# Two-part float32r operands for the probabilities and values of a sparse attention branch

## The chip, the cores and the metric

The kernel runs on one core of one Trainium2 chip. The core has a matrix engine (PE; its weight loads are listed apart as PEld), a vector engine (DVE), a scalar engine (ACT), a general engine (POOL) and a sync engine (SP) that issues most DMA transfers. Each engine works through its own fixed list of instructions in order; between engines only semaphores order the work. The metric is the device time of one execution in microseconds (us); a profile of one further execution shows where the time goes.

## The reference

One decoder block over 512 tokens of width 1024: a modulated RMS norm, a wide input projection, two token mixers side by side (NSA, a sparse attention with three branches, and MLA, a latent attention), their gated merge, an output projection and a squared-ReLU MLP. The part that matters here is NSA: 8 heads in 2 groups of 4, head width 64, blocks of 128 queries, three softmax branches that each have their own keys and values, weighted by gates:

```
p_cmp = masked_softmax(s, dist_c >= 0)
o_cmp = jnp.einsum('bghqk,bgkd->bghqd', p_cmp.astype(vc.dtype), vc)
...
p = masked_softmax(s, smask[:, :, None])
o_sel = jnp.einsum('bghqk,bgqkd->bghqd', p.astype(vs.dtype), v_sel)
...
p = masked_softmax(s, wmask)
o_win = jnp.einsum('bghqk,bgkd->bghqd', p.astype(vw.dtype), v_win)
o = g[0] * o_cmp + g[1] * o_sel + g[2] * o_win
```

With 512 tokens the 8 selectable blocks of 64 keys are always all chosen and the window of 512 reaches back to the first token, so the second and third branch are both causal attention over all keys, with different keys and values. The compressed branch has 31 block keys and values, made by a small MLP (weights w_c1, w_c2) from the tokens.

## The kernel before, in words

Features lie on the partitions and tokens along the free axis. Every large product is written with operands split in two float32r parts (a rounded copy, made on ACT, and the remainder, made on DVE), as three matmuls of 512 columns: lines 197, 198 and 199 in `mm3`. A dense unit, `z_unit`, is 8 x 3 = 24 such matmuls into one of two PSUM banks `acc`.

The attention products do without this split for the probabilities. `nsa_scores(hl)` makes, for head `hl` of both groups, the scores of both causal branches (L543, L544, L550, L551), the softmax (DVE L344 adds the bias and takes the minimum, ACT L346 takes the exponential, `normalise` multiplies by the gated reciprocal: DVE L369, ACT L367). `nsa_values(hl, sc)` then, for each branch, transposes the probabilities of both groups on PE (L391, ten 128 x 128 transposes for one group and branch, into two PSUM banks `t`), copies them to SBUF on DVE (L379, tile `pT`, three buffers) and multiplies them with the values in plain float32 (L568). In a product the stationary operand is 64 columns wide; group 0 writes the upper 64 partitions of the single bank `o`, group 1 the lower 64. The trace has two records for one plain float32 matmul, and its names give 128*64 for one of these. The compressed branch has products of its own: `cmp_values` (L519, two matmuls of 512 columns in bank `m`, added to the head's output by DVE L521). The profile's L568 and L519 rows together are what I call the value products.

The program is written as a list of steps, `ORDER`; each letter is one function, a number its argument: `s1` is `nsa_scores(1)`, `v1` `nsa_values(1, ...)`, `w1` `cmp_values(1)`, `c` `cmp_softmax`, `h` `hidden` (the MLP of the compressed branch, L435), `g`, `q`, `k` dense units of gates and of MLA's latents, `p`, `a`, `b`, `m` the MLA steps. A scheduler then lays each engine's instructions out, earlier steps first, but lets later ones run ahead where buffers and inputs are there. Tiles of a pool with the same tag share a ring of buffers: `N` (20), `X` (8), `C` (3), `tmp` (5), `pT` (3), `p` (5, one per head, group and branch).

Of the kernel before, what the change touches and what calls it, by code (L numbers as in the profile page):

```python
# [10 lines left out]
F32R = mybir.dt.float32r  # L11
BF16 = mybir.dt.bfloat16
AF = mybir.ActivationFunctionType
ALU = mybir.AluOpType
PSUM = bass.MemoryType.PSUM

P = 128
S = 512
# [13 lines left out]
PB = dict(acc=2, s=2, t=2, o=1, m=1)  # L32
NB = dict(raw=4, hi=3, lo=3, p=5, pT=3, qst=2, tmp=5, N=20)
LJ = True
# [7 lines left out]
NA = ["1"]  # L42
ORDER = "f0 t0 s0 t1 f1 h v0 c s1 v1 s2 g1 v2 g1 q w0 s3 w2 v3 w1 k g1 p g1 g1 a1 w3 a0 b1 a2 e1 b0 a3 m1 b3 e1 m3 m0 g1 b2 m2"


@with_exitstack
def block_kernel(ctx: ExitStack, tc: tile.TileContext, d):
# [12 lines left out]

    big_a = slot("A", 16)    # modulated input, merged mixer output, modulated MLP input
    big_x = slot("X", 8)     # residual, attention outputs
    big_n = slot("N", NB["N"])    # attention operands, channel gates, MLP hidden
    small_c = slot("C", 3)
# [6 lines left out]

# [1 line left out]
    def wtile(shape=(P, 1024)):  # L73
# [38 lines left out]
    def scale_col(out, col, k, g):  # L112
        """(1 + scale) * gain, for a column of scales"""
        nc.vector.scalar_tensor_tensor(out[:, k:k + 1], mod[:, col:col + 1], badd[:, (k if g == C_GMIX else 8 + k):(k if g == C_GMIX else 8 + k) + 1],
                                       cols[:, g + k:g + k + 1], op0=ALU.add, op1=ALU.mult)
# [4 lines left out]

# [1 line left out]
    class Stats:  # L122
        """Sums of squares per token over feature tiles; the last tile goes straight to the tensor engine."""

# [23 lines left out]
        def rstd(self, tag="m", tag2="m", tok=ALL):  # L148
# [12 lines left out]
            nc.vector.reciprocal(r, s)  # L161
            # one Newton step for the square root: s <- s / 2 + (v / 2) / s
            nc.vector.tensor_tensor(v, v, r, op=ALU.mult)
# [6 lines left out]

# [1 line left out]
    def wsplit(src, shape, far=False):  # L172
# [33 lines left out]

# [1 line left out]
    for j, c0 in enumerate((0, 24)):  # L208
# [3 lines left out]
    st0 = Stats(KT)  # L212
    # the condition's row on all partitions
    pcs = [psum("t") for _ in range(2)]
# [3 lines left out]
    for k in range(KT):  # L218
        st0.add(xt[k], k == KT - 1)
        # keeps the tensor engine's clock up until the first projection  # L220
        if k in WARM:
            nc.tensor.matmul(warm, ones, xt[k], start=True, stop=True)
        if k in (CB0, CB0 + 1):
            j = k - CB0
            nc.scalar.activation(cb[:, j * S:(j + 1) * S], pcs[j], AF.Copy)
# [44 lines left out]

# [1 line left out]
    distm = big_n("distm")  # L272
# [5 lines left out]

    # keys: float32r parts of one group and both branches, each part on both halves of the partitions
    kh = [sb.tile([P, 2, S], F32R, name=f"kh{g}", tag="kk", bufs=4) for g in range(2)]  # L280
# [22 lines left out]

    # rope key, on all partitions: the sum of its two products
    rsel = sb.tile([64, P], F32, name="rsel", tag="rep", bufs=2)
# [5 lines left out]

    # gates, token-major: [tok, tile, 24]
    gates = sb.tile([P, NQ, 24], F32, name="gates")
# [12 lines left out]

    # values of the selected and window branches, token-major
    vt = {}

    def v_tiles(br):  # L330
        pz = z_unit(2 + br)
        zv = tmp("zv")
        nc.scalar.activation(zv, pz, AF.Copy)
        pt = psum("m")
        for kb in range(NQ):
            nc.tensor.transpose(pt[:, kb * P:(kb + 1) * P], zv[:, kb * P:(kb + 1) * P], ident)
        v = big_n(f"v{br}")
        nc.vector.tensor_copy(v, pt)
        vt[br] = v

# [1 line left out]
    def soft(pp, n, bias, scale, o, nm, sm):  # L342
        """exp of one row block: pp holds the negated scores"""
        nc.vector.tensor_tensor_reduce(out=o, in0=pp, in1=bias[:, S - n:S], scale=scale, scalar=3e38,  # L344
                                       op0=ALU.add, op1=ALU.min, accum_out=nm)
        nc.scalar.activation(o, o, AF.Exp, bias=nm, scale=-1.0, accum_out=sm)  # L346
# [34 lines left out]
    def p_transposed(aps):  # L381
        """P^T per key block: [keys, q from the block's first row on]"""
        out = [None] * NQ
# [14 lines left out]

# [1 line left out]
    def flat_tiles(b):  # L400
# [7 lines left out]
        for half in range(2):  # L408
            fl = big_n(f"flat{b}{half}").rearrange("p (m g b) -> p m g b", m=8, g=2)
            nc.gpsimd.memset(fl[:, :, :, 31:32], 0.0)  # L410
            for g in range(2):
                # token 16 b + 2 m for block b and pair m
                src = cz[g][:, 16 * half:16 * half + 496].rearrange("p (b m two) -> p m b two", b=31, two=2)
# [7 lines left out]
    kcp = sb.tile([P, 64], F32, name="kcp")  # L421
    vcp = big_n("vcp").rearrange("p (r c) -> p r c", r=4)
    hid = {}

    def hidden(fk, fv):
        """keys on the first 64 rows, values on the others: (kv, g, block) x 256"""
        nc.sync.dma_start(w2, d["w_c2"])
# [24 lines left out]
        for g in range(2):  # L452
            nc.scalar.activation(kcp[64 * g:64 * g + 64, 32 * g:32 * g + 32], pk[64 * g:64 * g + 64, 0:32],
                                 AF.Copy, scale=0.5)
        pv = psum("m")
        nc.gpsimd.memset(vcp, 0.0)
        for g in range(2):
# [6 lines left out]
        for r in range(4):  # L464
            nc.vector.tensor_scalar(vcp[32 * r:32 * r + 32, r], pv[32 * r:32 * r + 32, 0:P], 0.5, None,
                                    op0=ALU.mult)

    # compressed branch: softmax over the 31 blocks for all heads of a q tile
    pct = [None, None]

    def cmp_softmax():
        """all heads of two q tiles at a time; columns (q tile, hl, g, block)"""
        dc = [big_n(f"biasc{i}") for i in range(2)]
        for i in range(2):
            nc.sync.dma_start(dc[i], d["biasc"][i])
        for g in range(2):
            pct[g] = big_n(f"pct{g}")
        for ii in range(2):
            pp = psum("m")
            for i2 in range(2):  # L480
                i = 2 * ii + i2
                for hl in range(4):
# [18 lines left out]
                                    op=ALU.mult)  # L501
            # rows (g, hl, block) for the transposes
            pc = tmp("pc")
# [9 lines left out]
            for g in range(2):  # L513
                nc.vector.tensor_copy(pct[g][:, 256 * ii:256 * ii + 256], pt[:, 256 * g:256 * g + 256])

    def cmp_values(hl):
        po = psum("m")
        for g in range(2):
            nc.tensor.matmul(po[64 * g:64 * g + 64, :], vcp[:, hl, 64 * g:64 * g + 64], pct[g],  # L519
                             start=True, stop=True, skip_group_check=True)  # L520
        nc.vector.tensor_tensor(o_sp[hl], o_sp[hl], po, op=ALU.add)  # L521

# [1 line left out]
    o_sp = [None] * 8  # L524
# [37 lines left out]
    def nsa_values(hl, sc):  # L562
        po = psum("o")
        for br in range(2):
            tr = [p_transposed(sc[2 * g + br]) for g in range(2)]
            for kb in range(NQ):
                for g in range(2):
                    nc.tensor.matmul(po[64 * g:64 * g + 64, kb * P:],  # L568
                                     vt[br][:, kb * P + 64 * g:kb * P + 64 * g + 64], tr[g][kb],
                                     start=(br == 0 and kb == 0), stop=(br == 1 and kb == 3), skip_group_check=True)  # L570
        o_sp[hl] = big_x(f"o{hl}")
        evac(o_sp[hl], po)

# [1 line left out]
    zq, cq, ckv = [], [], []  # L575
# [81 lines left out]

# [1 line left out]
    tab = {}  # L659
# [13 lines left out]

    # columns of modb: (sc_a k, sh_a k) pairs, gt_a, (sc_m k, sh_m k) pairs, gt_m
    GTA, SCM, GTM = 16, 24, 40
# [12 lines left out]
    def ada_fill(end):  # L688
        """modulation columns up to pair end"""
        while ai[0] < min(end, 24):  # L690
            ada_late(ai[0])
            ai[0] += 1

    mqk, msc, lat = {}, {}, {}
    for step in ORDER.split():
# [15 lines left out]
        elif op == "c":  # L711
            cmp_softmax()
        elif op == "w":
            cmp_values(a)
        elif op == "p":
# [13 lines left out]

    # attention outputs in two parts, in the room of the keys and probabilities  # L730
    oh = []
# [12 lines left out]

# [1 line left out]
    nc.vector.tensor_scalar(modb[:, GTA:GTA + 8], modb[:, GTA:GTA + 8], 0.5, None, op0=ALU.mult)  # L746
# [21 lines left out]
    for n in range(KT - NH1):  # L768
# [3 lines left out]
        out_tile(n, pa, ALL)  # L772
    # the last tiles by halves of the tokens, so that the next norm of one runs beside the products of the other
    for k in range(KT):
# [18 lines left out]

# [1 line left out]
    st2 = Stats(KT, -1)  # L795
# [91 lines left out]
def _prep(inp):  # L887
# [4 lines left out]
    out["crow"] = asc(a["c"])  # L892
    # modulation columns: (sc_a, sh_a) by tile, gt_a, (sc_m, sh_m) by tile, gt_m
    order = []
# [70 lines left out]
```

## Time and profile before

| | |
|---|---|
| Median of 3 runs | 839.21 us (837.82 to 839.64) |
| Profiled execution, span from first to last instruction | 834.8 us |
| Median minus span | 4.4 us |
| PE busy in the span | 810.3 us (97%) |
| DVE busy | 494.0 us (59%) |
| ACT busy | 324.2 us (39%) |
| Granted PE clock | full in nearly every slice of the span |

The profile takes down one execution by itself, so the span is not the same thing as a run's time: 4.4 us lie around it. Busy PE time counts from a matmul's start to its modelled end, and matmuls overlap; how fast PE really goes is read from the distance of one start to the next. Times along the span are counted from its start.

### The profile page before, as it was taken

What the parts mean: (1) busy time and instruction counts of PE and PEld (TensorE: products, weight loads), DVE (VectorE), ACT (ScalarE), POOL (GpSimd) and SP (SyncE); (2) the same over time, 40 slices, a digit from 0 to 9 for tenths busy, and PEclk for the clock granted to TensorE, in tenths of its full rate; (3) what the DMA queues carried; (4) which work ended last, traced back from release to release, by engine and by line L of the source; (5) the groups of instructions that cost most, each with busy time, mean ns of one, the idle gap of its engine ahead of it and who ended that gap; (6) DMA issues with size and microseconds to landing.
All of it is one profiled execution on the core that took longest, in us unless ns stands there. A gap on an engine that the chain in (4) does not pass through costs nothing.

```text
span 834.8 us, 10364 instructions
## 1 busy us (share of the span) xinstructions
PE 810.3 (97%) x3916; PEld 631.5 (76%) x3916; DVE 494.0 (59%) x964; ACT 324.2 (39%) x572; POOL 88.2 (11%) x71
## 2 busy tenths in 40 slices
PE   6899999999999999999989999999999999999996
PEld 3687668665577656888769998888888888888885
DVE  6979668878658875468777745333333334333434
ACT  4458427465315543222333444224321342223431
POOL 2500000000000000003320013002200220012100
PEclk9999999999999999999999999999999999999998
DMA  9683251010041123487656203223333223333203
GB/s 348 237 278 114 95 184 51 26 51 26 26 149 54 51 78 119 158 285 239 207 177 226 102 26 121 87 97 102 101 101 97 87 94 101 102 101 100 78 1 101
DMA packets 30996, 99.66 MB, mean 119 GB/s; under 512 B 3521, under 2 KB 5761, under 8 KB 30946
## 3 DMA queue, kind: packets, MB, share of 16 engines
q1 hardware_dynamic: 30880, 98.89, 35.9%
q8 instruction: 31, 0.51, 0.2%
q14 instruction: 19, 0.16, 0.1%
q0 software_dynamic: 64, 0.11, 0.0%
q10 hardware_dynamic: 2, 0.00, 0.0%
HBM read 96.89 MB, written 2.10 MB: 119 GB/s over the span
## 4 chain that ended last, share of the span: by engine, by line
PE 83%; DVE 8%; DMA 4%; issue 2%; POOL 1%; ACT 1%; SPq 0%; DVEq 0%; POOLq 0%; ACTq 0%
PE ps_acc L197 14%; PE ps_acc L199 13%; PE ps_acc L198 13%; PE ps_s L197 8%; PE ps_s L198 7%; PE ps_s L199 7%; PE ps_t L391 4%; PE ps_o L568 3%; DVE junk L107 3%; DMA w_raw<-in_w_ada_dram 3%; PE ps_s L640 2%; PE ps_o L653 2%; POOL yb L758 1%; PE ps_acc L267 1%; PE ps_s L267 1%
## 5 line engine op out<-in xcount | busy, mean ns | idle before, releaser
L183 ACT ACTIVATE w_hi<-w_raw 128x1024 fp32r<-128x1024 f32 x105 | 111.0, 1059 | 293.1 <-PE ps_acc L198 158.3
L184 DVE TENSOR_TENSOR w_lo<-w_raw,w_hi 128x1024 fp32r<-128x1024 f32 x105 | 128.3, 1223 | 106.1 <-ACT w_hi L183 102.8
L198 PE MATMUL ps_s<-ul,w_hi 128*128 128x512 f32 (+1 forms) x264 | 99.4, 377 | 0.0
L197 PE MATMUL ps_s<-uh,w_hi 128*128 128x512 f32 (+1 forms) x264 | 99.4, 377 | 0.0
L199 PE MATMUL ps_s<-uh,w_lo 128*128 128x512 f32 (+1 forms) x264 | 99.3, 376 | 0.0
L197 PE MATMUL ps_acc<-h2h,w_hi 128*128 128x512 f32 x224 | 87.1, 389 | 0.0
L198 PE MATMUL ps_acc<-h2l,w_hi 128*128 128x512 f32 x224 | 87.1, 389 | 0.0
L199 PE MATMUL ps_acc<-h2h,w_lo 128*128 128x512 f32 x224 | 87.1, 389 | 0.0
L828 POOL TENSOR_TENSOR relu<-relu 128x512 f32<-128x512 f32 x32 | 48.4, 1515 | 308.6 <-ACT relu L823 296.8
L798 DVE SCALAR_TENSOR_TENSOR xr<-ps_s,modb,xr 128x512 f32<-128x512 f32 (+1 forms) x35 | 24.7, 705 | 95.0 <-PE ps_s L199 94.9
L198 PE MATMUL ps_acc<-hl,w_hi 128*128 128x512 f32 x200 | 80.1, 401 | 0.0
L199 PE MATMUL ps_acc<-hh,w_lo 128*128 128x512 f32 x200 | 80.0, 400 | 0.0
L197 PE MATMUL ps_acc<-hh,w_hi 128*128 128x512 f32 x200 | 79.4, 397 | 0.0
L346 ACT ACTIVATE p<-p,nm 128x128 f32<-128x128 f32 (+3 forms) x96 | 53.3, 556 | 58.1 <-DVE nm L344 56.9
L379 DVE COPY pT<-ps_t 128x512 f32<-128x512 f32 (+1 forms) x72 | 42.4, 598 | 30.6 <-PE ps_o L568 16.1
L198 PEld LDWEIGHTS ps_s<-ul,w_hi 128*128 128x128 f32 x264 | 49.7, 188 | 9.5 <-DVE ul L829 0.4
L197 PEld LDWEIGHTS ps_s<-uh,w_hi 128*128 128x128 f32 x264 | 49.7, 188 | 9.2 <-DVE xr L798 0.2
L199 PEld LDWEIGHTS ps_s<-uh,w_lo 128*128 128x128 f32 x264 | 49.7, 188 | 9.0
L107 DVE SCALAR_TENSOR_TENSOR junk<-w_raw,cb 128x1024 bf16<-128x1024 f32 x32 | 40.1, 1254 | 14.7 <-DMA w_raw<-in_w_ada_dram 14.6
L198 PEld LDWEIGHTS ps_acc<-h2l,w_hi 128*128 128x128 f32 x224 | 42.0, 188 | 8.8
L197 PEld LDWEIGHTS ps_acc<-h2h,w_hi 128*128 128x128 f32 x224 | 42.0, 188 | 8.7
L199 PEld LDWEIGHTS ps_acc<-h2h,w_lo 128*128 128x128 f32 x224 | 42.0, 188 | 8.7
(387 smaller groups left out, 1458.1 us busy)
## 6 DMA issues: line engine op xcount, KB each, us to landing
w_raw<-in_w_fc_dram SPq DMA_DIRECT2D x64, 512.0 KB, 3.4
w_raw<-in_w_ada_dram SPq DMA_DIRECT2D x32, 512.0 KB, 4.2
w_raw<-in_w_z_dram SPq DMA_DIRECT2D x25, 512.0 KB, 3.7
w_ada<-in_w_ada_dram SPq DMA_DIRECT2D x16, 512.0 KB, 5.7
w_raw<-in_w_c_dram SPq DMA_DIRECT2D x8, 512.0 KB, 3.9
w_raw<-in_w_o_dram SPq DMA_DIRECT2D x8, 512.0 KB, 4.2
w_raw<-in_w_out_dram SPq DMA_DIRECT2D x8, 512.0 KB, 3.5
w_raw<-in_w_g_dram SPq DMA_DIRECT2D x8, 448.0 KB, 6.5
```

The source lines that it names most:

```text
L107: nc.vector.scalar_tensor_tensor(junk, w, 1.0, cb, op0=ALU.mult, op1=ALU.mult, accum_out=mod[:, col:col + 1])
L183: nc.scalar.activation(hi[:, :n], raw[:, :n], AF.Copy)
L184: nc.vector.tensor_tensor(lo[:, :n], raw[:, :n], f(hi[:, :n]), op=ALU.subtract)
L197: nc.tensor.matmul(out, w[0], x[0], start=first, stop=False)
L198: nc.tensor.matmul(out, w[0], x[1], start=False, stop=False)
L199: nc.tensor.matmul(out, w[1], x[0], start=False, stop=last)
L346: nc.scalar.activation(o, o, AF.Exp, bias=nm, scale=-1.0, accum_out=sm)
L379: nc.vector.tensor_copy(dst, src)
L391: nc.tensor.transpose(pp[:, off:off + P], aps[i][:, kb * P:(kb + 1) * P], ident)
L568: nc.tensor.matmul(po[64 * g:64 * g + 64, kb * P:], vt[br][:, kb * P + 64 * g:kb * P + 64 * g + 64], tr[g][kb], start=(br == 0 and kb == 0 ...
L798: nc.vector.scalar_tensor_tensor(xt[n][:, tok], pa[:, tok], modb[:, GTM + n:GTM + n + 1], xt[n][:, tok], op0=ALU.mult, op1=ALU.add)
L828: nc.gpsimd.tensor_tensor(r2, r, r, op=ALU.mult)
```

## The change

The probabilities and the values of the NSA branches now go through float32r as well. Each transposed probability tile is split in two parts, `pTh` by ACT and `pTl` by DVE (L423 and L424 of the new file), the values of each branch and group are kept as one tile in which the two parts of V lie side by side (64 + 64 columns per key block), and a product is two float32r matmuls with a stationary operand of 128 columns: one for `pTh`, one for `pTl` (L602). The upper half of the output bank holds the sums with V's first part, the lower half those with its second. The compressed branch's probabilities are split the same way and are added in the same accumulation (L606), so that `cmp_values` and the `w` steps are gone. At the end ACT copies the lower half out and DVE adds the upper (L610, L611). A group has a whole bank to itself now, so the single bank `o` is used once for each head and group (eight times) instead of once for each head pair. `c` moves ahead of `v0`. `pT` gets four buffers, and a split tile takes two of them; `N` gets 19. Comments are taken out as well.

```diff
-NB = dict(raw=4, hi=3, lo=3, p=5, pT=3, qst=2, tmp=5, N=20)
+NB = dict(raw=4, hi=3, lo=3, p=5, pT=4, qst=2, tmp=5, N=19)
-ORDER = "f0 t0 s0 t1 f1 h v0 c s1 v1 s2 g1 v2 g1 q w0 s3 w2 v3 w1 k g1 p g1 g1 a1 w3 a0 b1 a2 e1 b0 a3 m1 b3 e1 m3 m0 g1 b2 m2"
+ORDER = "f0 t0 s0 t1 f1 h c v0 s1 v1 s2 g1 v2 g1 q s3 v3 k g1 p g1 g1 a1 a0 b1 a2 e1 b0 a3 m1 b3 e1 m3 m0 g1 b2 m2"
+    def value_parts(name, src, get):
+        v = get(name, F32R)
+        v4 = v.rearrange("p (kb part c) -> p kb part c", part=2, c=64)
+        nc.scalar.activation(v4[:, :, 0], src, AF.Copy)
+        nc.vector.tensor_tensor(v4[:, :, 1], src, f(v4[:, :, 0]), op=ALU.subtract)
+        return v
...
-        v = big_n(f"v{br}")
-        nc.vector.tensor_copy(v, pt)
-        vt[br] = v
+        src = pt.rearrange("p (kb g c) -> p kb g c", kb=NQ, g=2)
+        vt[br] = []
+        for g in range(2):
+            vt[br].append(value_parts(f"v{br}{g}", src[:, :, g], big_n))
...
+    def p_parts(aps):
+        out = [None] * NQ
+        for grp in ((0,), (1, 3), (2,)):
+            pp = psum("t")
...
+            th = sb.tile([P, S], F32R, name="pTh", tag="pT", bufs=NB["pT"])
+            tl = sb.tile([P, S], F32R, name="pTl", tag="pT", bufs=NB["pT"])
+            nc.scalar.activation(th[:, :off], pp[:, :off], AF.Copy)
+            nc.vector.tensor_tensor(tl[:, :off], pp[:, :off], f(th[:, :off]), op=ALU.subtract)
...
-    vcp = big_n("vcp").rearrange("p (r c) -> p r c", r=4)
+    vc = [small_c(f"vc{g}", F32R) for g in range(2)]
...
+        for g in range(2):
+            v4 = vc[g].rearrange("p (r part c) -> p r part c", r=4, part=2)
+            src = vcp[:, :, 64 * g:64 * g + 64]
+            nc.scalar.activation(v4[:, :, 0], src, AF.Copy)
+            nc.vector.tensor_tensor(v4[:, :, 1], src, f(v4[:, :, 0]), op=ALU.subtract)
...
-                nc.vector.tensor_copy(pct[g][:, 256 * ii:256 * ii + 256], pt[:, 256 * g:256 * g + 256])
+                to, of = slice(256 * ii, 256 * ii + 256), pt[:, 256 * g:256 * g + 256]
+                nc.scalar.activation(pct[g][0][:, to], of, AF.Copy)
+                nc.vector.tensor_tensor(pct[g][1][:, to], of, f(pct[g][0][:, to]), op=ALU.subtract)
...
     def nsa_values(hl, sc):
-        po = psum("o")
-        for br in range(2):
-            tr = [p_transposed(sc[2 * g + br]) for g in range(2)]
-            for kb in range(NQ):
-                for g in range(2):
-                    nc.tensor.matmul(po[64 * g:64 * g + 64, kb * P:],
-                                     vt[br][:, kb * P + 64 * g:kb * P + 64 * g + 64], tr[g][kb],
-                                     start=(br == 0 and kb == 0), stop=(br == 1 and kb == 3), skip_group_check=True)
         o_sp[hl] = big_x(f"o{hl}")
-        evac(o_sp[hl], po)
+        for g in range(2):
+            po = psum("o")
+            for br in range(2):
+                tr = p_parts(sc[2 * g + br])
+                for kb in range(NQ):
+                    for t in tr[kb]:
+                        nc.tensor.matmul(po[:, kb * P:], vt[br][g][:, kb * P:(kb + 1) * P], t,
+                                         start=(br == 0 and kb == 0 and t is tr[0][0]), stop=False,
+                                         skip_group_check=True)
+            for t in pct[g]:
+                nc.tensor.matmul(po, vc[g][:, hl * P:(hl + 1) * P], t, start=False, stop=(t is pct[g][1]),
+                                 skip_group_check=True)
+            r = slice(64 * g, 64 * g + 64)
+            u = tmp("osum")
+            nc.scalar.activation(u[r], po[64:P], AF.Copy)
+            nc.vector.tensor_tensor(o_sp[hl][r], po[0:64], u[r], op=ALU.add)
```

The scheduler lays the engines' lists out anew. On PE, in the values of the second head pair (`v1`), the list before had this (`v_794` is the second branch's values, `kh` and `kl` keys, `ident` the identity of a transpose; the scores are the third pair's):

```order
L391 MATMUL ps_t<-ident,p 128x128 x2
L568 MATMUL ps_o<-pT,v_794 64x512
L391 MATMUL ps_t<-ident,p 128x128 x8
L550 MATMUL ps_s<-kh_509,qst 128x512
L551 MATMUL ps_s<-kl_511,qst 128x512
L543 MATMUL ps_s<-kh_510,qst 128x256
L544 MATMUL ps_s<-kl_512,qst 128x256
L391 MATMUL ps_t<-ident,p 128x128 x2
L568 MATMUL ps_o<-pT,v_794 64x512
L568 MATMUL ps_o<-pT,v_794 64x384
```

In the same place of the new list stand these (`v_641` is the first branch's values of group 0):

```order
L419 MATMUL ps_t<-ident,p 128x128 x7
L602 MATMUL ps_o<-pTh,v_641 128x512
L419 MATMUL ps_t<-ident,p 128x128 x2
L602 MATMUL ps_o<-pTl,v_641 128x512
L602 MATMUL ps_o<-pTh,v_641 128x384
L602 MATMUL ps_o<-pTl,v_641 128x384
L602 MATMUL ps_o<-pTh,v_641 128x256
L419 MATMUL ps_t<-ident,p 128x128 x4
L602 MATMUL ps_o<-pTl,v_641 128x256
L602 MATMUL ps_o<-pTh,v_641 128x128
L602 MATMUL ps_o<-pTl,v_641 128x128
```

A product for `pTh` follows ACT's copy, the next for `pTl` follows DVE's remainder, and only transposes stand between them. From the last product of the first head's group 0 to the last of the third head pair the new list holds five dense matmuls, all at the start; the list before has 63 dense matmuls from the first product of `v1` to the last of `v2`.

ACT takes the results of dense units out of the two `acc` banks. In the list before, the first latent unit `cqz` leaves its bank (L583, and L130 for its squares) ahead of the softmax of the fourth head pair (`qn_535`):

```order
L367 ACTIVATE p<-p,rc 128x256 x2
L183 ACTIVATE w_hi<-w_raw 128x1024
L583 ACTIVATE cqz_1601<-ps_acc 128x512
L130 ACTIVATE sq<-ps_acc 128x512
L346 ACTIVATE p,sm<-p,nm 128x128 x2
L346 ACTIVATE p,sm<-p,nm 128x256 x2
L346 ACTIVATE p,sm<-p,nm 128x384 x2
L346 ACTIVATE p,sm<-p,nm 128x512
L534 ACTIVATE qst<-qn_535 64x512
```

In the new list it leaves after the last `osum` of the third head pair:

```order
L423 ACTIVATE pTh<-ps_t 128x512
L356 ACTIVATE p,sm<-p,nm 128x384
L423 ACTIVATE pTh<-ps_t 128x512
L423 ACTIVATE pTh<-ps_t 128x256
L356 ACTIVATE p,sm<-p,nm 128x512 x2
L610 ACTIVATE osum<-ps_o 64x512
L622 ACTIVATE cqz_1771<-ps_acc 128x512
L130 ACTIVATE sq<-ps_acc 128x512
L622 ACTIVATE cqz_1806<-ps_acc 128x512
L130 ACTIVATE sq<-ps_acc 128x512
```

Both banks `acc` hold latent units until then.

## Rows read from the trace of the kernel before

**Rows 1.** The page's head: span, then busy time, share, instructions per engine.
```profile
span 834.8 us, 10364 instructions
...
PE 810.3 (97%) x3916; PEld 631.5 (76%) x3916; DVE 494.0 (59%) x964; ACT 324.2 (39%) x572; POOL 88.2 (11%) x71
...
PEclk9999999999999999999999999999999999999998
```
**Rows 2.** The page's chain that ended last, share by engine.
```profile
PE 83%; DVE 8%; DMA 4%; issue 2%; POOL 1%; ACT 1%; SPq 0%; DVEq 0%; POOLq 0%; ACTq 0%
```
**Rows 3.** Stretches: length, busy us per engine, granted clock, DMA share, GB/s.
```profile
92.30:226.85 134.55, 133.57 (x711) 86.44 (x711) 100.47 (x282) 65.47 (x154) 4.43 (x8) 1.00 0.21 71
147.70:163.70 16.00, 15.87 (x90) 9.23 (x89) 12.47 (x40) 6.72 (x22) 0.00 (x0) 1.00 0.09 30
```
**Rows 4.** PE in order of time: start, length, record; the value products.
```profile
149.62 1.07 PE L568 MATMUL ps_o<-pT,v 128*64 128x512 f32 x4
150.62 0.44 PE L550 MATMUL ps_s<-kh,qst 128*128 128x384 f32 x1
...
151.48 0.86 PE L568 MATMUL ps_o<-pT,v 128*64 128x384 f32 x4
152.27 0.66 PE L391 MATMUL ps_t<-ident,p 128*128 128x128 f32 x4
...
162.12 0.86 PE L568 MATMUL ps_o<-pT,v 128*64 128x256 f32 x6
162.91 1.09 PE L391 MATMUL ps_t<-ident,p 128*128 128x128 f32 x8
```
**Rows 5.** The same view: float32r matmuls of 512, 384 and 256 columns.
```profile
157.91 0.28 PE L543 MATMUL ps_s<-kh,qst 128*128 128x256 f32 x1
158.03 0.28 PE L544 MATMUL ps_s<-kl,qst 128*128 128x256 f32 x1
...
161.44 0.34 PE L550 MATMUL ps_s<-kh,qst 128*128 128x384 f32 x1
161.62 0.34 PE L551 MATMUL ps_s<-kl,qst 128*128 128x384 f32 x1
161.79 0.40 PE L198 MATMUL ps_acc<-hl,w_hi 128*128 128x512 f32 x1
...
164.31 0.39 PE L198 MATMUL ps_acc<-hl,w_hi 128*128 128x512 f32 x1
164.54 0.39 PE L199 MATMUL ps_acc<-hh,w_lo 128*128 128x512 f32 x1
```
**Rows 6.** Groups by line and shape: count, busy us, mean ns, idle before.
```profile
L379 DVE COPY pT<-ps_t 128x512 f32<-128x512 f32 x48 | 32.8, 687 | 25.0 <-PE ps_o L568 12.5 <-PE ps_t L391 7.2 <-PE ps_o L653 4.7
...
L346 ACT ACTIVATE p<-p,nm 128x512 f32<-128x512 f32 x24 | 17.2, 718 | 8.4 <-DVE nm L344 8.1
...
L344 DVE CUSTOM_DVE_ANT_0 p<-ps_s,distm 128x512 f32<-128x512 f32 x16 | 10.8, 686 | 1.7 <-PE ps_s L551 1.7
...
L289 DVE TENSOR_TENSOR kl<-ps_t,kh 64x512 fp32r<-64x512 f32 x8 | 5.5, 686 | 0.1
...
L287 ACT ACTIVATE kh<-ps_t 64x512 fp32r<-64x512 f32 x8 | 4.7, 590 | 0.1
```
**Rows 7.** DVE in order of time: a copy of 256 columns and what follows.
```profile
161.23 0.42 DVE L379 COPY pT<-ps_t 128x256 f32<-128x256 f32 x1 [0.35 <-PE ps_o L568]
161.57 1.00 DVE L369 TENSOR_SCALAR p<-p,rc 128x128 f32<-128x128 f32 x3
```
**Rows 8.** Waits from 92.3 to 226.85: us in total, times, longest.
```profile
PEld ps_o L568 <- DVE pT L379: 3.2, 8, 0.6
...
PEld ps_t L391 <- DVE pT L379: 1.5, 4, 0.8
```
**Rows 9.** The w_c1 products' matmuls, shortest, median, longest ns, first and last start.
```profile
L435 PE MATMUL ps_m<-w_raw,flat x64: 379/379/431, 92.3 to 107.7; 128*64 128x256 f32 x64
```
**Rows 10.** The chain from 92 to 109 us: start, length, what.
```profile
96.96 3.95 DMA w_raw<-in_w_c_dram
```

More of the change, by code (lines that the diff above doesn't have):

```diff
@@ L397, in p_transposed @@
         return out
+    def p_parts(aps):
+        out = [None] * NQ
+        for grp in ((0,), (1, 3), (2,)):
+            pp = psum("t")
+            off = 0
+            pos = []
+            for kb in grp:
+                pos.append(off)
+                for i in range(kb, NQ):
+                    nc.tensor.transpose(pp[:, off:off + P], aps[i][:, kb * P:(kb + 1) * P], ident)
+                    off += P
+            th = sb.tile([P, S], F32R, name="pTh", tag="pT", bufs=NB["pT"])
+            tl = sb.tile([P, S], F32R, name="pTl", tag="pT", bufs=NB["pT"])
+            nc.scalar.activation(th[:, :off], pp[:, :off], AF.Copy)
+            nc.vector.tensor_tensor(tl[:, :off], pp[:, :off], f(th[:, :off]), op=ALU.subtract)
+            for kb, o in zip(grp, pos):
+                out[kb] = [t[:, o:o + (NQ - kb) * P] for t in (th, tl)]
+        return out
     def flat_tiles(b):
@@ L455, in hidden @@
         pv = psum("m")
+        vcp = tmp("vcp").rearrange("p (r c) -> p r c", r=4)
         nc.gpsimd.memset(vcp, 0.0)
@@ L476, in cmp_softmax @@
         for g in range(2):
-            pct[g] = big_n(f"pct{g}")
+            pct[g] = [big_x(f"pct{part}{g}", F32R) for part in "hl"]
         for ii in range(2):
@@ L513, in cmp_softmax @@
             for g in range(2):
-                nc.vector.tensor_copy(pct[g][:, 256 * ii:256 * ii + 256], pt[:, 256 * g:256 * g + 256])
-    def cmp_values(hl):
-        po = psum("m")
-        for g in range(2):
-            nc.tensor.matmul(po[64 * g:64 * g + 64, :], vcp[:, hl, 64 * g:64 * g + 64], pct[g],
-                             start=True, stop=True, skip_group_check=True)
-        nc.vector.tensor_tensor(o_sp[hl], o_sp[hl], po, op=ALU.add)
+                to, of = slice(256 * ii, 256 * ii + 256), pt[:, 256 * g:256 * g + 256]
+                nc.scalar.activation(pct[g][0][:, to], of, AF.Copy)
+                nc.vector.tensor_tensor(pct[g][1][:, to], of, f(pct[g][0][:, to]), op=ALU.subtract)
     o_sp = [None] * 8
@@ L562, in nsa_values @@
     def nsa_values(hl, sc):
-        po = psum("o")
-        for br in range(2):
-            tr = [p_transposed(sc[2 * g + br]) for g in range(2)]
-            for kb in range(NQ):
-                for g in range(2):
-                    nc.tensor.matmul(po[64 * g:64 * g + 64, kb * P:],
-                                     vt[br][:, kb * P + 64 * g:kb * P + 64 * g + 64], tr[g][kb],
-                                     start=(br == 0 and kb == 0), stop=(br == 1 and kb == 3), skip_group_check=True)
-        o_sp[hl] = big_x(f"o{hl}")
-        evac(o_sp[hl], po)
+        o_sp[hl] = big_x(f"o{hl}")
+        for g in range(2):
[14 more added lines that the diff above has]
+            nc.vector.tensor_tensor(o_sp[hl][r], po[0:64], u[r], op=ALU.add)
     zq, cq, ckv = [], [], []
@@ L712, in block_kernel @@
             cmp_softmax()
-        elif op == "w":
-            cmp_values(a)
         elif op == "p":
```

## The prediction

> **What bounds the kernel now.** I read the page's head first: PE is busy 97% of the span at full granted clock, DVE 59%, ACT 39% [rows 1]. The chain that ended last runs over PE for 83% of its length [rows 2]. Then the stretches. The value products of NSA lie between the first w_c1 product (L435, 92.30) and the first product of MLA's w_uv (226.85), 134.55 us in which PE is busy 133.57, DVE 100.47 and ACT 65.47 [rows 3]. Inside `v1` it is the same: PE 15.87 of 16.00, DVE 12.47, ACT 6.72 [rows 3].
>
> A busy PE may still be slack, so I priced its instructions from one start to the next in the time-ordered view of `v1`. A float32r matmul takes 0.23 at 512 columns (164.31 to 164.54), 0.18 at 384 (161.44 to 161.62), 0.12 at 256 (157.91 to 158.03) [rows 5]; a transpose 0.11, from (1.09 - 0.66) / 4 [rows 4]. A plain float32 product of 512 columns takes 1.00 (149.62 to 150.62), a pair that starts with 384 columns 0.79, one that starts with 256 columns 0.79 [rows 4]. Going into and out of such a block costs besides: the matmul that follows it has a record of 0.44 where one of its shape has 0.34 [rows 4, 5], and the block at 162.12 starts 0.33 after a 512-column matmul that should take 0.23 [rows 4, 5]. So 0.19 a block for both. At these prices all work of the stretch comes to 128.7 of its 134.55 us, and 5.8 are stalls: PE does bound it.
>
> The Trainium skill (Perfetto Trace Analysis, section Identifying the Most-Contended Engine) would have me judge PE by its busy weight loads, not by matmuls. They are 86.44 of 134.55, 64% [rows 3], below DVE's 75%; by that DVE is the bound and the change, which leaves DVE's work as it is, gives nothing: 839. The pitches speak against it. It is part of rival B.
>
> **The change part by part.** *Removed on PE.* For one head pair and branch the products take 1.00 + 1.00 + 0.79 + 0.80 = 3.59; eight of these are 28.7. L519 gives five blocks of 1.00 in the stretch, 5.0. The list has 36 blocks, x 0.19 = 6.9. Sum 40.6; two more L519 blocks stand behind the stretch, 2 x 1.19 = 2.4. Removed: 43.0.
>
> *Added on PE.* For one head, group and branch: two parts of four matmuls, 2 x (0.228 + 0.175 + 0.121 + 0.11) = 1.27; sixteen make 20.3. The compressed branch adds 16 x 0.228 = 3.6. Sum 23.9. No row shows float32r at 128 columns: a quarter of 0.23 is 0.06, and the 256-column price 0.12 is the other bound. I take the transpose's 0.11; the 32 matmuls move the sum by -1.7 to +0.3. PE's net: 43.0 - 23.9 = 19.1 us less.
>
> *DVE.* Where it copied `pT` (687 ns for 512 columns) it now subtracts, and a subtraction from PSUM of that size takes 686 [rows 6]: nothing. Eight `osum` additions (0.69) take the place of four copies of `o` and four additions of L521: nothing.
>
> *ACT.* New are 32 copies of 512 columns at 0.59 (L287 [rows 6]), 16 of 256 at about 0.34 (a little over half), 8 `osum` at 0.59 and some 3 us for V and the compressed probabilities: 18.9 + 5.4 + 4.7 + 3 = 32 us. ACT goes from 65 to 97 in the stretch, below PE. No cost by itself, as long as the queues don't cross.
>
> *Where they do cross.* I cut the new PE list at the same marks into five pieces and priced each.
> - A, the w_c1 products with group 0 of `v0`: PE 12.9. But the weights set this piece: a transfer of 3.95 us stands on the chain at 96.96 [rows 10], and the products run from 92.3 to 107.7 [rows 9]. 15.7 as before.
> - B, `c`, scores and 91 dense matmuls: PE 29.9, DVE 28, ACT 21. With about half the old stalls 33.
> - C, the rest of `v0` with all of `v1` and `v2`: 86 transposes, 92 value products, 34 scores and five dense matmuls, PE 32.4. DVE: 28 remainders and 6 additions, 18 x 0.69 + 10 x 0.42 + 6 x 0.69 = 20.8 [rows 6, 7]; 26 masks, 0.69 at 512 columns and in proportion below, 12; 15 multiplications at about 0.4, 6; small ones 6. The records add up to 45, but neighbours overlap: a copy of 0.42 starts at 161.23 and the next instruction at 161.57, 0.08 before its end [rows 7]. Some 90 such places take off 7: DVE 38. ACT 33.5. So C is no longer PE's: DVE decides. No dense work covers it, since both `acc` banks hold latent units until ACT reaches L622. At each of six head ends PE stops, ACT takes 0.59 for `osum`, and DVE waits for that: 6 x 0.6 = 3.6. C is 42.
> - D, 72 dense matmuls with `v3`: PE 30.1, DVE 23, ACT 23; with the other half of the stalls 32.
> - E, the way to w_uv: PE 6.8, taken as 7.3.
>
> Sum 130.0. The same work took 134.55 + 2.4 = 136.9. So -6.9: PE's 19.1 lose 12 to the places where DVE, ACT or a transfer is late next.
>
> *Edits at nothing.* `N` 19: the MLP behind needs fewer. `pT` 4: the MLA steps share it and had three. The C ring: `vc0` and `vc1` hold two of its three buffers until `v3` is done, so SP's qt_rope transfers wait, and behind them the later weights; the uqk loads stand ahead in SP's queue and some 25 us of dense work cover them. Without that cover it costs a transfer, 4 us [rows 10]; I keep that for the upper end. The single bank `o`, used eight times in place of four: the bank is free after ACT 0.59 + DVE 0.69, with 0.8 us of transposes between; in C that is within DVE's time.
>
> The profiled execution is 834.8, the median 4.4 above it. 834.8 - 6.9 + 4.4 = 832.3 us.
>
> **Rivals.**
> *A: all of PE's saving arrives.* For it: DVE has 34 us of room in the stretch and the softmax of the next pair can run ahead of the values. Against: in C only five dense matmuls stand, and DVE's 38 alone are over PE's 32.4. With C at 36 and B, D without stalls the sum is 15.7 + 30 + 36 + 30.1 + 7 = 118.8, -18.1: 821.1.
>
> *B: nothing changes.* For it: if DVE and ACT, not PE, set the pace in C (at 48 to 49), the piece eats the saving: 88.0 + 48.9 = 136.9. Also if the changed products cost more than by the pitches. Against: before, DVE was the one that waited, its 512-column copies 12.5 us for L568 and 7.2 for transposes [rows 6]. 839.
>
> *C: slower, by the hand-over in piece C.* Each split group is a chain: four transposes (0.44), ACT's `pTh` (0.59), DVE's `pTl` (0.69), and only then the last product and a free buffer. Before, one copy stood there (0.69), and PE had dense matmuls to run meanwhile. If nothing overlaps, 18 groups of 512 columns take 1.72 and 10 of 256 take 0.22 + 0.34 + 0.42 = 0.98: 40.8. On each of the two engines stand softmax instructions ahead (0.72 and 0.69 at 512 columns [rows 6], some 0.45 over all widths); half of one on each adds 0.45 per group, 12.6. C is 53.4, the sum 141.4, +4.5: 843.7. It decides from 48.9, that is from (48.9 - 40.8) / 28 = 0.29 us of queueing per group without any overlap. For it: ACT waited 8.1 for DVE's `nm` and DVE 1.7 for scores [rows 6], so these queues already cross. Against: there are two banks `t`, so that one group's transposes run beside another's copies, and before PE waited for `pT` only 3.2 us in 8 places at the products and 1.5 in 4 at the transposes [rows 8].
>
> The Trainium skill (Perfetto Trace Analysis, section Optimization Strategy) says that a gap which repeats on the engine that should be full can mean too few buffers. The trace of before shows it only in those 4.7 us; after, a split group holds two of four `pT`, so the rule would back this rival.
>
> **How the numbers follow.** About 0.2% (1.7 us) is what a measurement of this kernel can tell from no change: 837.5 to 840.9. The forecast, with C from 37 to 47, has 0.55 and its own range 824 to 837.5; A 0.13; B 0.13; C 0.19, spread from 841 upward. Faster: 0.55 + 0.13 = 0.68; same 0.13; slower 0.19. A's lower half and C's upper half are left out: the range is 820 to 844, which holds qt_rope's 4 us above the forecast too.
>
> **What would show it.** The 128-column L602 at a pitch of 0.11, no 0.10 of going in and out at the products; the way from the first w_c1 product to the first w_uv product 128 to 131 us in place of 134.55; ACT up by about 32 there and DVE's busy time as before. In piece C PE is idle with `pTh` and `pTl` (L423, L424) as releasers and DVE over 85% busy. Behind the w_uv mark everything keeps its length, but for the two blocks. I am wrong on the place if PE waits mainly outside C or on transfers; wrong on the pace if C is under 37 or over 47; and wrong on the price if L602's pitches differ from those of the scores.

## The result, and the profile after

The changed kernel takes 848.63 us (median of 4, 847.76 to 853.15) against 838.52 before: a ratio of 1.0137 with a 95% interval of 1.0116 to 1.0158. It is slower by 10 us where I forecast 7 faster. The profiled execution's span is 845.9 against 834.8. First the head of the changed kernel's page and the shares of its chain that ended last [rows 1, 2]:

```profile
span 845.9 us, 10462 instructions
...
PE 802.5 (95%) x3916; PEld 645.6 (76%) x3916; DVE 495.5 (59%) x968; ACT 353.7 (42%) x638; POOL 90.7 (11%) x71
...
PE 72%; DVE 11%; issue 6%; DMA 4%; ACT 4%; POOL 2%; SPq 0%; DVEq 0%; POOLq 0%; ACTq 0%
```

PE is busy 8 us less; ACT 30 us more and DVE about the same, both near the forecast. But the chain now leaves PE for 28% of the span instead of 17%. To see where, I cut the span at the marks of the prediction: first w_c1 product, last product of the hidden layer, first product of the compressed branch (L606), last one of the third head pair, first w_uv product, first product of the MLP behind. These are pieces A, B, C, D with E, and MLA (columns as in [rows 3]):

```profile
92.58:110.39 17.81, 15.51 (x115) 10.22 (x115) 8.07 (x22) 8.92 (x21) 0.20 (x1) 1.00 0.65 218
110.39:144.31 33.92, 33.21 (x184) 27.72 (x181) 29.07 (x83) 20.36 (x48) 2.78 (x4) 1.00 0.33 108
144.31:188.37 44.06, 38.21 (x217) 28.67 (x217) 36.55 (x108) 33.89 (x88) 1.22 (x2) 1.00 0.05 16
188.37:236.15 47.78, 41.98 (x208) 32.65 (x207) 29.39 (x75) 30.03 (x61) 1.98 (x2) 0.96 0.15 45
236.15:481.75 245.60, 236.07 (x1134) 184.18 (x1135) 170.56 (x330) 84.50 (x151) 20.60 (x12) 0.99 0.47 152
```

| piece | forecast | measured | over |
|---|---|---|---|
| A | 15.7 | 17.8 | +2.1 |
| B | 33 | 33.9 | +0.9 |
| C | 42 | 44.1 | +2.1 |
| D and E | 39.3 | 47.8 | +8.5 |
| MLA, to the MLP behind | 241.1 | 245.6 | +4.5 |

(241.1 is 243.5, the way from 226.9 to 470.3 before, less the two L519 blocks.) The sum over is 18.1; the span is 18.0 over the forecast 827.9. Piece C, where I had put the risk, came out 2 us off. The loss stands behind it, in D, E and MLA. There PE stands still; the time-ordered view of PE, idle time and its releaser in brackets:

```profile
189.42 0.27 PE L419 MATMUL ps_t<-ident,p 128*128 128x128 f32 x1
190.87 0.50 PE L197 MATMUL ps_acc<-hh,w_hi 128*128 128x512 f32 x1 [1.18 <-ACT sq L130]
...
219.81 0.53 PE L602 MATMUL ps_o<-pTl,v 128*128 128x384 f32 x1 [0.93 <-DVE pTl L424]
...
225.43 0.40 PE L606 MATMUL ps_o<-pctl,vc 128*128 128x512 f32 x1
227.62 0.50 PE L197 MATMUL ps_acc<-hh,w_hi 128*128 128x512 f32 x1 [1.79 <-ACT sq L130]
...
236.15 0.50 PE L197 MATMUL ps_acc<-w_hi,ckv0h 128*128 128x512 f32 x1 [1.44 <-ACT ckv0h L192]
...
237.49 0.50 PE L199 MATMUL ps_acc<-w_hi,ckv0l 128*128 128x512 f32 x1 [0.61 <-DVE ckv0l L193]
...
239.47 0.50 PE L197 MATMUL ps_acc<-w_hi,ckv0h 128*128 128x512 f32 x1 [0.79 <-DVE vm L389]
...
258.31 0.47 PE L197 MATMUL ps_acc<-cq0h,w_hi 128*128 128x512 f32 x1 [2.22 <-DVE km L389]
...
261.40 0.50 PE L197 MATMUL ps_acc<-cq0h,w_hi 128*128 128x512 f32 x1 [0.79 <-DVE qm L669]
```

Two of these stops (190.87 and 227.62) end with ACT's `sq`. ACT in order of time says why:

```profile
225.86 0.59 ACT L610 ACTIVATE osum<-ps_o 64x512 f32<-64x512 f32 x1 [1.63 <-PE ps_o L606]
226.48 0.60 ACT L622 ACTIVATE ckvz<-ps_acc 128x512 f32<-128x512 f32 x1
226.97 0.59 ACT L130 ACTIVATE sq<-ps_acc 128x512 f32<-128x512 f32 x1
227.45 0.61 ACT L622 ACTIVATE ckvz<-ps_acc 128x512 f32<-128x512 f32 x1
```

`v3` stands ahead of `k` in `ORDER`, and its last `osum` stands ahead of `k`'s `ckvz` in ACT's list, and PE waits with both `acc` banks full. The first of them has been ready for some 20 us, since this product, the last of its unit:

```profile
206.35 0.39 PE L199 MATMUL ps_acc<-hh,w_lo 128*128 128x512 f32 x1
```

ACT had time in between (it stands idle 3.34 us up to 221.99, 1.63 before that `osum`); what keeps the bank full is the place in the list. In the kernel before, the values had nothing on ACT, and its trace has the same drain in the midst of `v3`:

```profile
210.06 0.58 ACT L583 ACTIVATE ckvz<-ps_acc 128x512 f32<-128x512 f32 x1
```

so that `v3`'s products covered the norm that follows (statistics, scaling, `ckv0h` at 222.69). Now this chain from 226.48 to 235.48 has 24 dense matmuls beside it, and PE runs dry at its end: `ckv0h`, `ckv0l`, `vm`.

The waits for `km` and `qm` have another cause. A gate unit's products end at 254.35, and ACT takes them out of their bank only here:

```profile
285.20 0.60 ACT L703 ACTIVATE tab<-ps_acc 128x512 f32<-128x512 f32 x1 [0.29 <-PE ps_acc L198]
```

For 31 us MLA has one `acc` bank. Before, the unit that stands there (its last product at 245.39) was out of its bank at 246.56. The ring `N` says why: at 254 `krs`, six parts of `cq`, four of `ckv`, four `vm` and the `tab` of four earlier gate units are all still to be read, 19 tiles in 19 buffers, and this `tab` is the twentieth. It is written right behind the last product that reads `ckv0l` (L198, the releaser in the row above), whose start is here:

```profile
284.77 0.39 PE L198 MATMUL ps_acc<-ckv0l,w_hi 128*128 128x512 f32 x1
```

### The profile page after: what moved, and what is told of

The parts are those of the page before. It is cut to its first block, busy times and chain, and to the rows that moved or that the text cites. A ratio compares the mean times of both kernels' runs of the same rounds, so it can differ in the third digit from the quotient of the medians.

```text
span 845.9 us, 10462 instructions
## 1 busy us (share of the span) xinstructions
PE 802.5 (95%) x3916; PEld 645.6 (76%) x3916; DVE 495.5 (59%) x968; ACT 353.7 (42%) x638; POOL 90.7 (11%) x71
## 4 chain that ended last, share of the span: by engine, by line
PE 72%; DVE 11%; issue 6%; DMA 4%; ACT 4%; POOL 2%; SPq 0%; DVEq 0%; POOLq 0%; ACTq 0%
PE ps_acc L197 13%; PE ps_acc L198 12%; PE ps_acc L199 12%; PE ps_s L197 7%; PE ps_s L198 7%; PE ps_s L199 7%; DMA w_raw<-in_w_ada_dram 3%; DVE junk L107 3%; PE ps_s L679 2%; PE ps_o L692 2%; POOL yb L795 1%; DVE pTl L424 1%; PE ps_o L602 1%; PE ps_t L401 1%; DVE w_lo L184 1%
## 5 line engine op out<-in xcount | busy, mean ns | idle before, releaser
L198 PE MATMUL ps_s<-ul,w_hi 128*128 128x512 f32 (+1 forms) x264 | 99.4, 377 | 0.0
L198 PE MATMUL ps_acc<-h2l,w_hi 128*128 128x512 f32 x224 | 87.1, 389 | 0.0
L198 PE MATMUL ps_acc<-hl,w_hi 128*128 128x512 f32 x200 | 79.8, 399 | 0.0
L198 PEld LDWEIGHTS ps_s<-ul,w_hi 128*128 128x128 f32 x264 | 49.7, 188 | 9.4 <-DVE ul L866 0.4
L198 PEld LDWEIGHTS ps_acc<-h2l,w_hi 128*128 128x128 f32 x224 | 42.0, 188 | 8.7
L197 PEld LDWEIGHTS ps_acc<-hh,w_hi 128*128 128x128 f32 x200 | 37.6, 188 | 13.3 <-ACT sq L130 3.7
```

Source lines behind the costliest of these rows:

```text
L197: nc.tensor.matmul(out, w[0], x[0], start=first, stop=False)
L198: nc.tensor.matmul(out, w[0], x[1], start=False, stop=False)
```

## The experiments

Theory 1: the loss is cover. PE's short products leave the latent norms and MLA's start uncovered, because the drains of the `acc` banks come late. Theory 2 (the rival of the prediction): the loss is the hand-over of the split groups, from transposes to ACT to DVE to product. Each kernel is the changed one with the edit shown; ratios are against the kernel before on the same chip.

**k_first**
```diff
-... g1 v2 g1 q s3 v3 k g1 p ...
+... g1 v2 g1 q s3 k v3 g1 p ...
```


> The changed kernel with only k moved ahead of v3. Theory 1: the waits behind v3 go (1.96, 1.60, 0.78, 0.95 and part of the 2.4 at km), that behind v2 (1.34) stays: 842 to 844. Theory 2: 847 to 849.

842.53, ratio 1.0054 (1.0033 to 1.0074): 6.1 us under the changed kernel. Piece C is as in the changed kernel (44.0), D with E shrinks from 47.8 to 37.5 (some 2.5 us of `v3`'s transposes and products now stand behind the mark, as cover for w_uv; the first `ckvz` is taken out at 208.89):

```profile
190.70:228.20 37.50, 36.02 (x190) 29.33 (x189) 27.89 (x72) 28.79 (x58) 1.97 (x2) 1.00 0.15 50
```

Theory 1 as expected.

**g_late**
```diff
-... p g1 g1 a1 a0 b1 a2 e1 b0 a3 m1 b3 ...
+... p g1 a1 a0 b1 a2 e1 b0 a3 m1 g1 b3 ...
```


> The changed kernel with one gate unit (a g1 behind p) moved back behind m1. In the changed kernel this unit's products end at 254.4 and ACT takes them out of the acc bank only at 285.2, so that MLA has one acc bank for 31 us, and PE waits 2.2 us for km, 0.8 for qm and a few times less. Theory 1 (cover and acc banks): with the bank free these waits go, 844 to 846.5. Theory 2 (only the hand-overs in the values): the same as the changed kernel, 847 to 849.

844.28, ratio 1.0083 (1.0050 to 1.0116), 4.3 us under, a gain that these few runs know only to some 3 us either way. MLA's piece falls from 245.6 to 243.0, and the waits for `km` and `qm` are not in its trace. (D with E has 50.2 in this profile, with PE at the lower of its two clock levels from 230 to 236 (granted clock 0.50); such spells are told of below.)

**kg_late**, both edits:

> Both moves: k ahead of v3, and the gate unit behind m1. Theory 1: the two gains add, k_first's 842.5 less some 3: 838 to 841. Theory 2: as k_first without more, 842 to 844.

836.79, ratio 0.9983 (0.9971 to 0.9995), 11.8 us under the changed kernel, a little below the range: the gains add (6.1 + 4.3) and a little more. Of the stops listed above, those for `sq` behind `v3`, for `ckv0h`, `ckv0l`, `km` and `qm` are not in its trace; that for `sq` behind `v2` (1.2) and one for `vm` (1.0) are. C and then D with E:

```profile
145.50:189.50 44.00, 38.16 (x217) 28.70 (x217) 36.50 (x108) 33.84 (x88) 1.22 (x2) 1.00 0.05 15
189.50:227.10 37.60, 36.12 (x190) 29.33 (x190) 28.00 (x73) 28.88 (x58) 1.96 (x2) 1.00 0.14 50
```

No product, split or hand-over of the change was touched: it is the same work in another order.

**n21_raw3**
```diff
-NB = dict(raw=4, hi=3, lo=3, p=5, pT=4, qst=2, tmp=5, N=19)
+NB = dict(raw=3, hi=3, lo=3, p=5, pT=4, qst=2, tmp=5, N=21)
```


> The changed kernel with the order of its steps, N at 21 tiles in place of 19, paid for with raw at 3 in place of 4 (one weight tile less ahead). If it is the N ring that keeps the gate unit in its acc bank from 254.4 to 285.2 (its tile tab finds no free buffer), the unit is taken out within 2 us of its last product and the waits for km and qm (3 us) go: 844 to 847, or more where the missing weight tile makes a transfer late. If something else on ACT keeps it, it stays some 30 us as it is.

848.28, ratio 1.0119 (1.0089 to 1.0149): no gain in time that shows, a miss, but the question is answered. The gate unit, whose last product here starts at 255.60, leaves its bank at once, and the waits for `km` and `qm` are gone:

```profile
256.76 0.58 ACT L703 ACTIVATE tab<-ps_acc 128x512 f32<-128x512 f32 x1
```

So it is the ring `N` that held the bank, as the count of its tiles says (`raw` changed too, but takes no part in that count). What the time lost again: in this profile PE ran at the lower clock level inside MLA's piece (the window from 470 to 476 has a granted clock of 0.50), which alone can take up to 3 us, as much as the waits were worth. That this is where the gain went is argued, not shown.

**qk_first**: `k` ahead of `v3` and `q` ahead of `v2`.

> The changed kernel with one line changed: in the list of steps the two latent steps stand ahead of the values beside them (q before v2, k before v3), so that ACT takes the latent units out of the acc banks and their norms run while the value products still stand on PE. Theory 1 (the loss is cover: PE stands still behind the last product of v2 and of v3 until ACT has drained the latent units, 1.34 and 1.96 us, and until ckv0h, ckv0l, vm and km are there, 1.60, 0.78, 0.95 and 2.4): these waits, some 9 us, mostly go, 839 to 842. Theory 2 (the loss is the hand-over of the split groups, transposes to ACT to DVE to product): the hand-overs are the same, 847 to 849.

843.74, ratio 1.0063 (1.0048 to 1.0079): better than the changed kernel but not below k_first, a miss. The stop behind `v2` went, and another took its place: with the dense units moved (73 dense matmuls in A and B where the changed kernel has 92), nothing stood beside the compressed softmax. PE stopped for 3.48 us, and the granted clock fell to the lower level in that stop and stayed there for 10.2 us ((0.39 + 0.46) x 6 / 0.5):

```profile
142.51 1.08 PE L548 MATMUL ps_m<-ident,pc 128*128 128x128 f32 x4 [3.48 <-DVE pc L542]
```
```profile
140.00:146.00 6.00, 2.34 (x6) 1.29 (x6) 3.53 (x10) 1.36 (x3) 0.00 (x0) 0.61 0.28 90
146.00:152.00 6.00, 5.07 (x17) 4.09 (x17) 2.59 (x6) 2.38 (x6) 0.00 (x0) 0.54 0.00 0
```

(The first is PE in order of time, the second windows of 6 us; the granted clock is the third number from the end.)

**one_part**
```diff
-            tl = sb.tile([P, S], F32R, name="pTl", tag="pT", bufs=NB["pT"])
-            nc.vector.tensor_tensor(tl[:, :off], pp[:, :off], f(th[:, :off]), op=ALU.subtract)
...
-                out[kb] = [t[:, o:o + (NQ - kb) * P] for t in (th, tl)]
+                out[kb] = [t[:, o:o + (NQ - kb) * P] for t in (th,)]
```


> The changed kernel without pTl: DVE's remainders (28 us of DVE in the stretch) and the products with them (10 us of PE) are left out, so the probabilities go in with one part alone; ACT's copies pTh stay, and the order of the steps too. Theory 2: with DVE's half of each hand-over gone the waits at the products in pieces C and D (some 14 us) go beside the 10 us of products: 824 to 828. Theory 1: the 10 us of products go, the waits for pTh and for the latent units stay: 835 to 840.

838.60, ratio 0.9990 (0.9971 to 1.0010): 10.0 us under, on theory 1's side, but the total alone doesn't decide, since the profile has two spells of 6.8 us at the lower clock (at 212 and 246) that can cost up to 3.4 each. The pieces do (C, then D with E):

```profile
142.70:177.00 34.30, 30.91 (x172) 22.43 (x172) 20.77 (x73) 29.35 (x79) 0.78 (x2) 1.00 0.07 27
177.00:223.20 46.20, 40.59 (x195) 31.82 (x194) 24.29 (x65) 31.65 (x65) 1.67 (x3) 0.93 0.16 46
```

C falls by 9.8 us, of which 5.8 are its 40 products less (0.228 + 0.175 + 0.12 + 0.06, over 4, each). D with E falls by 1.6 where 16 products less are worth 2.3, and its spell can cost up to 1.7 more than the one in the changed kernel: with half of every hand-over gone, nearly all of the loss there is still there. So this half of the hand-over has about 4 us in C and at most 1 us behind it.

**th_dve**
```diff
-            nc.scalar.activation(th[:, :off], pp[:, :off], AF.Copy)
+            nc.vector.tensor_copy(th[:, :off], pp[:, :off])
```


> The changed kernel with pTh copied by DVE instead of ACT: ACT loses 24 us in the stretch, DVE gains 28. Theory 2: a group's chain is longer by 0.1 us and all of it on the engine that decides piece C; C grows by the 14 us of DVE work that falls into it: 856 to 865. If it is ACT's queue that is in the way (theory 1 in its ACT form), the latent units leave earlier and part of this comes back: 848 to 854.

862.69, ratio 1.0286 (1.0234 to 1.0337): in theory 2's range, and what theory 1 in its ACT form expected did not come. With 24 us less on ACT the latent unit leaves no earlier; ACT stands idle for 6 us and still takes it out only behind `v3`'s last `osum`:

```profile
237.11 0.59 ACT L610 ACTIVATE osum<-ps_o 64x512 f32<-64x512 f32 x1 [6.01 <-PE ps_o L606]
237.72 0.60 ACT L622 ACTIVATE ckvz<-ps_acc 128x512 f32<-128x512 f32 x1
```

So it is not ACT's load that is in the way behind C, but the order of its list. In C DVE is busy 51.38 of 54.2 us; with 14.8 us more of DVE's work C is 10.1 longer. DVE had 7.5 us of air in C (44.06 less 36.55), no more.

**kg_pipe** puts the remainder products one group later (written in `nsa_values`: products of group n's `pTh`, then of group n-1's `pTl`).

> As kg_late, and the products of the remainders pTl are put one group later, behind the pTh products of the next group, so that PE doesn't wait for ACT and DVE within one group. The same instructions, in another order on PE. If the waits for pTl in piece C (some 4 us) and the half-clock spells behind them are the hand-over's, they go: 3 to 6 us under kg_late. If C is bound by DVE's sum of work (38 of its 44 us), C keeps its length and kg_late's time stands.

837.36, ratio 0.9998 (0.9983 to 1.0012): no gain, C is 45.8. The waits for `pTl` were not what set C; in C the chain runs over DVE and ACT. Of the changed kernel's chain in C, by line:

```profile
by line: DVE pTl L424 21.6%; DVE p L354 12.0%; ACT pTh L423 9.2%; ACT p L356 8.2%; DVE p L379 8.1%; PE ps_t L419 7.8%; PE ps_o L602 7.8%; issue 6.2%; ACT osum L610 4.1%; DVE o L611 3.1%; ACT w_hi L183 2.4%; PE ps_o L606 2.4%; DVE qst L566 2
```

**kg_spread** moves the gate unit behind `v2` (a `g1`) to between `v0` and `s1`.

> As kg_late, with a gate unit put between v0 and s1, so that dense matmuls of its 24 can stand in piece C where PE waits. If the loss in C is want of cover, 2 to 4 us under kg_late; if DVE's work sets C, PE's dense work there is done beside it and C is no longer, and what stands behind is shorter by the same: also 2 to 4 us under. If ACT and DVE have no room for the unit's w_hi, w_lo and tab, no gain or a loss: kg_late's time to 3 us over.

838.83, ratio 0.9996 (0.9978 to 1.0014): no gain, 2 us over kg_late, in the third case's range.

**kg_noscale, kg_na13, kg_pool** take DVE's multiplications by the reciprocals away (but for ACT's one), move the fourth query block's to ACT, or the first's to POOL (all three in kg_late's order; the last two in MLA's softmax as well).

> As kg_late, without DVE's multiplication of the NSA probabilities by the gated reciprocals (three of four query blocks stay unscaled; ACT's share stays): DVE has about 6 us less in piece C and the softmax is a step shorter. If DVE sets C (its busy time is 36.5 of 44), C falls by 4 to 6 us and the time to 831 to 833; if C is the length of the hand-over chains, by 1 to 2 us: 834 to 836.

> As kg_late, with the fourth query block's multiplication (512 columns) on ACT instead of DVE: DVE loses some 2.4 us in piece C, ACT (33.8 of 44) gains some 3.3. If DVE sets C: 1 to 2 us less, 835 to 836; if ACT and DVE together (each group passes both) set it: no change or 1 us more, 837 to 838.

> As kg_late, with the multiplication of the first query block (128 columns) on POOL instead of DVE. DVE loses some 1.4 us in piece C. If DVE sets C: 1 us less at most, unless POOL's own time comes into the chain to the transposes, which costs as much again: 835 to 838.

836.66, 837.15 and 839.04, ratios 1.0005 (0.9987 to 1.0023), 1.0004 (0.9992 to 1.0017) and 1.0022 (1.0007 to 1.0038). The first and the last lie outside all that was expected of them. None is faster than kg_late, so nothing here speaks for DVE's sum as what sets C. They don't settle it either: the lists came out differently (245 PE records between C's marks in kg_noscale, 217 in kg_late) and PE ran part of that way at the lower clock (0.96 over C in kg_noscale, 0.93 in kg_na13).

## Why the prediction was wrong

The step that failed is "D ... with the other half of the stalls 32", with E "taken as 7.3". I priced both by PE's own work (30.1 and 6.8) and a share of the old stalls, 2.4. What I left out is that the copies new on ACT put the latent norm behind `v3`, where before it ran beside `v3`'s products, so that nothing but one dense unit covers it. The stops listed above are 1.2 and 1.8 for `sq`, 1.4 for `ckv0h` and 0.9 for `pTl`, and the spell at the lower clock costs up to 1.7: 7.0 in all, where I had 2.4; the rest of the 8.5 over is in small stops, most of them at the hand-overs of `v3`. kg_late has neither the stop behind `v3`, nor the one for `ckv0h`, nor the spell, and shows 37.6; with the 2.5 us that stand behind its mark that is 40.1, near the 39.3. I had seen the late drain, and the prediction says that the banks hold latent units until L622. I counted it as lack of cover in C and not as a delay of what follows.

The second is "Edits at nothing: `N` 19: the MLP behind needs fewer". I counted the tiles of the MLP and not those of MLA, where 20 are alive at once; the gate's `tab` found no buffer, and an `acc` bank stood full for 31 us: 4.4 of the 4.5 us over in MLA are the stops listed above (`ckv0l`, `vm`, `km`, `qm`), 3.0 of them for `km` and `qm`, which n21_raw3 and g_late remove, and 1.4 for the late norm.

By the prediction's own sign I was wrong on the place: the costly waits stand outside C, and what lies behind the w_uv mark did not keep its length.

The rest by its steps:
- *What bounds the kernel:* PE by the pitches; no run speaks against that for the kernel before. In the changed kernel no engine is full from C to E. The rule of the Trainium skill (Perfetto Trace Analysis, section Identifying the Most-Contended Engine), by which the change would have given nothing, came nearer to the time than I did, but not by its reason: DVE is busy 36.55 of 44.06 in C and 29.39 of 47.78 behind it.
- *PE's net:* near. Nothing shows the 0.10 of going in and out at the products; 256 columns take 0.12, as priced, and 128 columns less than taken, 0.05 and 0.12 for a pair where I had 0.22:

```profile
159.66 0.28 PE L602 MATMUL ps_o<-pTh,v 128*128 128x256 f32 x1
159.78 0.28 PE L602 MATMUL ps_o<-pTl,v 128*128 128x256 f32 x1
159.90 0.22 PE L602 MATMUL ps_o<-pTh,v 128*128 128x128 f32 x1
159.95 0.28 PE L602 MATMUL ps_o<-pTl,v 128*128 128x128 f32 x1
160.07 0.45 PE L606 MATMUL ps_o<-pcth,vc 128*128 128x512 f32 x1
```
- *DVE and ACT sums:* near. From A to E DVE is busy 103.1 (the pieces' sum) for 100.5 before, ACT 93.2 for 65.5: 28 more where I had 32. The split group by group:

```profile
L424 DVE TENSOR_TENSOR pTl<-ps_t,pTh 128x512 fp32r<-128x512 f32 (+1 forms) x48 | 28.0, 598 | 11.9 <-ACT pTh L423 11.4
...
L423 ACT ACTIVATE pTh<-ps_t 128x512 fp32r<-128x512 f32 (+1 forms) x48 | 24.5, 521 | 18.2 <-PE ps_t L419 13.1 <-PE ps_o L602 2.4 <-DVE pTl L424 2.2
```
- *Piece C:* 44.1 for 42; DVE busy 36.55 for 38, 83% where I asked for 85. Rival C, slower by the hand-over, came out on the right side and nearest in its time (843.7, 4.9 under), but not by its mechanism: its deciding point, C at 48.9, wasn't reached. The queue that cost was ACT's, by its order, and it cost behind C. The Trainium skill (Perfetto Trace Analysis, section Optimization Strategy) let one expect a gap that repeats, for want of buffers. The gaps that cost most stand alone; the ring that ran short behind them was `N`, not `pT`. Small gaps that repeat are there in C:

```profile
PEld ps_t L419 <- DVE pTl L424: 3.0, 8, 0.5
...
PE ps_o L602 <- DVE o L611: 1.9, 4, 0.7
```

(Waits in C: us, times, longest. `pTl` is the last to read a bank `t`, `o` the last to read the bank `o`.)
- *A:* 2.1 over. PE waits 0.92 for `flat` (DVE), and 0.86 and 0.41 for w_c1 transfers; in kg_late one such wait is 2.5.
- *qt_rope:* hidden, as forecast; no stop names it.

What stays open: what sets C, which no edit made shorter than 44 except by leaving work out (no run gave `t`, `o` or `pT` another buffer, so their waits remain a rival); why the scheduler put the drain behind `osum`, beyond that it moves with `k`; and the clock spells, which I could not place. kg_late's profile (836.2) is 8.3 over the forecast's 827.9: 3.3 in A, 0.9 in B, 2.0 in C, 1.9 behind. So with both causes gone the change gives 1.5 us where I had forecast 7. (The kernel before was not run with its steps in kg_late's order; it has none of the waits that this order removes.)

## What to carry to other kernels

When a change makes one engine's work shorter and gives another more, ask what ran beside that work, and follow this chain to its end: the price shows up behind the change, in a stage that it doesn't touch. When work is put on an engine that had none in a step, look for what now stands behind it in that engine's list, above all the copies that free a PSUM bank. And the size of a ring is judged at the stage where most of its tiles are alive at once, here MLA; a tile without a buffer keeps a PSUM bank full.

## What the runs showed of the hardware

- Plain float32 blocks cost 0.19 us to enter and leave, but transposes between float32r matmuls nothing: in the changed kernel four of them take 0.36 (156.26 to 156.62) and the product of 256 columns behind them 0.20 in place of 0.12, together what four pitches of 0.11 and one of 0.12 make:

```profile
156.26 0.60 PE L419 MATMUL ps_t<-ident,p 128*128 128x128 f32 x4
156.62 0.36 PE L602 MATMUL ps_o<-pTl,v 128*128 128x256 f32 x1
156.82 0.22 PE L602 MATMUL ps_o<-pTh,v 128*128 128x128 f32 x1
```

- Beside some stops of PE stands a spell at the lower clock, which can cost more than the stop. In the kernel before the granted clock is 1.00 all the way from 92 to 227 [rows 3]. In runs with stops of 1 to 4 us there are spells at the lower level (1.2 instead of 2.4 GHz) close behind some of them. The changed kernel, after the stops at `v3`'s second group:

```profile
212.00:218.00 6.00, 5.66 (x37) 4.29 (x35) 3.38 (x7) 3.29 (x7) 0.00 (x0) 1.00 0.20 58
218.00:224.00 6.00, 5.03 (x22) 3.64 (x20) 3.30 (x5) 2.00 (x5) 0.00 (x0) 0.72 0.29 90
```
```profile
215.53 0.93 PE L419 MATMUL ps_t<-ident,p 128*128 128x128 f32 x7
...
221.09 1.72 PE L419 MATMUL ps_t<-ident,p 128*128 128x128 f32 x7
```

(Windows of 6 us, then PE in order of time: the same seven transposes at both levels.) 0.28 x 6 / 0.5 is 3.4 us. Not every stop has such a spell (kg_late's of 1.2 and 1.0 have none), and its place isn't the same in two runs, so its price can only be told run by run; that the stop brings it on is not shown.
